# Strassen's seven products in two pieces of each down product of a hybrid decoder layer

## The chip, the cores and the metric

The kernel runs on 1 core of one Trainium2 chip. The metric is the device time of one execution, in microseconds (us). Three runs of the kernel before took 743.64 to 743.83 us, with a median of 743.7 us. The core has five engines with a queue of their own each: PE (TensorE, matmuls; its weight loads are listed as PEld), DVE (VectorE), ACT (ScalarE), POOL (GpSimd) and SP (SyncE, which here issues the loads of the weights). [...]

## The reference

One decoder layer on x of 1 x 256 x 1024, all F32. Three sub-layers follow each other, each between two RMS norms:

```python
def swiglu(x, w_gate, w_up, w_down):
    return (jax.nn.silu(x @ w_gate) * (x @ w_up)) @ w_down
...
h = h + 0.5 * rmsnorm(swiglu(rmsnorm(h, ffn1_pre_g), ffn1_w_gate, ffn1_w_up, ffn1_w_down), ffn1_post_g)
u = rmsnorm(h, mix_pre_g)
z, xbc, dt_raw, q, k, v, gate_logits = split(u @ w_in)
y_ssd = ssd_branch(z, xbc, dt_raw, ...)       # convolution, chunked state space (32 heads), gated norm, projection
y_att = diff_attn_branch(q, k, v, ...)        # differential attention, 8 heads, projection
h = h + rmsnorm((gates[0] * y_ssd + gates[1] * y_att) @ w_out, mix_post_g)
h = h + 0.5 * rmsnorm(swiglu(rmsnorm(h, ffn2_pre_g), ffn2_w_gate, ffn2_w_up, ffn2_w_down), ffn2_post_g)
```

The inner width of both SwiGLUs is 2816. The down product `@ w_down`, which the change touches, multiplies 256 x 2816 by 2816 x 1024.

## The kernel before

**Precision.** Every large product is made of fp32r matmuls. A value is split in two: `hi` is the value rounded to fp32r and `lo` is what is left. A product of two split values is taken as three matmuls, hi*hi, lo*hi and hi*lo. Weights are split on the way: ACT casts the F32 chunk to hi (`L168`), DVE subtracts hi from the chunk for lo (`L171`). Each chunk of 1 MB gives two pairs of such instructions, each of 128 x 1024.

**Weights.** All weights of the layer are listed in order of use as chunks of 128 partitions x 2048. SP loads them into three raw buffers (`load_to`, `L147`); a raw buffer goes back to SP when its last split has read it. `take()` hands the next chunk to the matmuls and sees to it that the splits of the two chunks behind it are written (`AHEAD = 3`). The split chunks live in tiles of 4 KB per partition of a pool called k4 (29 buffers), which also holds the activations, the gains and more. A pool k3 of 4 buffers of 3 KB holds tiles of the SSD branch (E) and of the attention (s); k2 (7 buffers of 2 KB) holds small ones. PSUM has 8 banks: 3 in the pool pj and 5 in the pool bg.

**A SwiGLU** (`ffn`). Gate and up products of 256 channels each (`mm_w`, into pj) are evicted by ACT and DVE, multiplied, and split into `gh` and `gl`, in which channels lie on partitions and the 256 tokens on the free axis. The down product (`mm_n`) then goes over 11 pieces of 256 channels, one weight chunk each. A piece is 24 matmuls of 128x128 by 128x512: 2 channel tiles, 2 token blocks, 3 terms, 2 halves of the outputs (`L470`). The four sums [token block][half] stay in four bg banks over all pieces. The last three pieces (`TAIL`) are held back, so that token block 0 is finished first: `ready(0)` then runs its norm (`post_norm`: square on ACT, product with the gain on DVE, rstd on POOL or ACT, addition to h on DVE) beside block 1's matmuls, and after the first SwiGLU the transposes for the next norm (`turned`, tile pu_mx) follow between block 1's matmuls.

**Order.** In the first products and in the tail of `mm_n` the order on some engines is that of the program (`own_order`). Elsewhere a planner decides, when the kernel is built, in which order each engine gets its instructions, from costs of its own. In the middle stage the work of the SSD branch and of the attention runs as background (`Background`): its pieces carry costs (`yield 1.4`) and come due while the projections z, q, k and the gates go on. At run time each engine works down its queue in the built order.

Of the kernel before, what the change touches and what calls it, by code (L numbers as in the profile page):

```python
# [11 lines left out]
F32 = mybir.dt.float32  # L15
# [9 lines left out]
P = 128  # L25
# [5 lines left out]
H_SSD = 32  # L31
H_ATT = 8
NEG = -1e30
K4_BUFS = 29
K3_BUFS = 4
K2_BUFS = 7
RAW_BUFS = 3
AHEAD = 3
# [3 lines left out]
BG_US = 3.15  # L42
GATE_US = 1.35
SSD_US = 1.55
BREAK, STOP = object(), object()


@with_exitstack
def tile_hybrid_layer(ctx: ExitStack, tc: tile.TileContext, x, ffn1_pre_g, ffn1_w_gate, ffn1_w_up,
# [33 lines left out]
    def bg(shape, name):  # L83
        return ps.tile(shape, F32, tag="bg", name=name, bufs=5)


    chunks = []

    def t_chunk(w, k0, c0):
        chunks.append((w[k0:k0 + D, c0:c0 + T].rearrange("(j p) c -> p j c", p=P), [P, KD, T]))  # L90

    def s_chunk(w, k0, c0):
        chunks.append((w[k0:k0 + 512, c0:c0 + 512].rearrange("(j p) c -> p j c", p=P), [P, 4, 512]))

    def n_chunk(w, k0):
        chunks.append((w[k0:k0 + 2 * P, :].rearrange("(j p) c -> p j c", p=P), [P, 2, D]))

    w_in2 = w_in[0]
    Z0, XS0, B0, C0, DT0, Q0, KK0, V0, G0 = 0, 2048, 4096, 4608, 5120, 5152, 6176, 7200, 8224
# [1 line left out]
    def ffn_chunks(wg, wu, wd):  # L101
        for w in (wg, wu):
            for k0 in (0, 512):
                s_chunk(w[0], k0, 0)
        for j in range(2, FF // T):
            t_chunk(wg[0], 0, j * T)
            t_chunk(wu[0], 0, j * T)
        for j in range(FF // T):
            n_chunk(wd[0], j * T)

    ffn_chunks(ffn1_w_gate, ffn1_w_up, ffn1_w_down)
    for c in range(2):
# [37 lines left out]
    def split_steps(ahead=True):  # L150


        i = len(splits)
        load_to(i + 1)
        r, shape = raws[i], chunks[i][1]
        nj = shape[1] // 2
        his, los = [], []
        splits.append((his, los))
        for q in range(2):
            hi = k4([P, nj, shape[2]], f"whi{i}{q}", F32R)  # L160
            lo = k4([P, nj, shape[2]], f"wlo{i}{q}", F32R)
            his.append(hi)
            los.append(lo)
            n = 1 if i == 0 else nj
            for j in range(0, nj, n):
                js = slice(j, j + n)
                copy = nc.scalar.copy if i + q + j else nc.vector.tensor_copy
                copy(hi[:, js, :], r[:, q * nj + j:q * nj + j + n, :])  # L168
                if not i + q + j:
                    yield  # L170
                nc.vector.tensor_sub(lo[:, js, :], r[:, q * nj + j:q * nj + j + n, :], hi[:, js, :].bitcast(F32))  # L171
                yield
        raws[i] = None
        if ahead:
            load_to(i + 1 + RAW_BUFS)

    def split_to(n):

        while len(splits) < min(n, len(chunks)):
            for _ in split_steps():  # L180
                pass

    def take(ahead=AHEAD):

        i = taken[0]
        taken[0] += 1
        split_to(i + ahead)
        his, los = splits[i]
        splits[i] = None
        nj = chunks[i][1][1] // 2  # L190
        return (lambda j: his[j // nj][:, j % nj, :], lambda j: los[j // nj][:, j % nj, :])

    def split(hi, lo, src):
# [259 lines left out]
        nc.gpsimd.dma_start(pg, v[0].partition_broadcast(P))  # L453
        return pg

    def mm_n(acc, acts, ready, turned, begun=lambda: None):


        n = len(acts) // 2
        held = []  # L460

        def one(i, w, parts):
            wh, wl = w
            for kt in range(2):
                ah, al = acts[2 * i + kt]
                for b, qs in parts:
                    ts = slice(b * P, (b + 1) * P)
                    for x_, w_ in ((ah, wh), (al, wh), (ah, wl)):
                        for q in qs:
                            nc.tensor.matmul(acc[b][q], x_[:, ts], w_(kt)[:, halves[q]],  # L470
                                             start=i == 0 and kt == 0 and x_ is ah and w_ is wh,
                                             stop=i == n - 1 and kt == 1 and w_ is wl)
                if i == 0:
                    begun()

        for i in range(n):
            w = take()
            if i < n - TAIL:
                one(i, w, ((0, (0, 1)), (1, (0, 1))))
            else:  # L480
                held.append((i, w))
        own_order(PE)
# [9 lines left out]
        split_to(taken[0] + AHEAD)  # L492
        ready(1)

    class Norm:

# [63 lines left out]
    def ffn(post_v, tag, ready, turned, then, products):  # L560
# [24 lines left out]
        back(1)  # L585
        del sgs
        then()
        for j in range(2, FF // T):
# [10 lines left out]
            nc.vector.tensor_tensor(sg, su, sg, ALU.mult)  # L599
            split(gh[:, o:o + 2, :], gl[:, o:o + 2, :], sg)  # L600
        if ready is store:
            act_table(EXP_LN)
        pg = load_gain(post_v, f"pg_{tag}")
        acc = [[bg([P, 512], f"acc_{tag}{b}{q}") for q in range(2)] for b in range(2)]
# [255 lines left out]
    cbm = [cbm2[g // 2][:, g % 2, :] for g in range(4)]  # L860

    def cb_work():
        for g in range(4):
            pc = bg([P, 3 * P], f"pcb{g}")
            nc.tensor.matmul(pc[:, P:], bT[:, g, :P], cT[:, g, :], start=True, stop=True)
            nc.tensor.matmul(pc[:, :P], bT[:, g, P:], cT[:, g, P:], start=True, stop=True)
            nc.vector.tensor_tensor(cbm[g], pc, m3.rearrange("p a b -> p (a b)"), ALU.mult)
            yield 0.5

# [207 lines left out]
    def att_work():  # L1077
# [4 lines left out]
        heads = [Head(hd, pairs[hd // 2]) for hd in range(H_ATT)]  # L1082
        for n in range(H_ATT // 2 + 2):
            here, old = heads[2 * n:2 * n + 2], heads[2 * n - 2:2 * n] if n else []
            for head in here:
                head.scores()
            for head in here:
                head.softmax()
                yield 2.3
            for head in old:  # L1090
                head.turn()
            if old and opens:
# [5 lines left out]
            if old:  # L1098
# [202 lines left out]
```

## Time and profile before

| what | value |
|---|---|
| median of 3 runs | 743.7 us |
| the profiled execution, and its span from first to last instruction | 743.95 us, 742.2 us |
| busy: PE / DVE / ACT / POOL | 734.1 / 525.2 / 441.1 / 38.0 us |
| first down product, from its first matmul | at 132.88 us |
| second down product, from its first matmul | at 676.16 us |
| granted TensorE clock, mean | 0.997 |

The page of the profile gives busy times by engine, the chain that ended last and the costliest groups of instructions. Every other view asks the same profiled execution: the chain in order of time has lines "start us, us, what"; the waits have lines "who waited <- for whom: us in total, times, longest us"; the timeline has lines "start us, us, engine, line, operation, out<-in xcount" and in brackets the idle time before it and what ended that. Lines such as L470 are lines of the kernel before.

### The profile page before, as it was taken

Reading aid. Unit: us, or ns where it says so; the run is one execution under the profiler, and the core shown is the slowest. Engines: PE = TensorE matmul, PEld = TensorE weight load, DVE = VectorE, ACT = ScalarE, POOL = GpSimd, SP = SyncE. Lnnn points to the kernel's source line nnn. Section 1 sums busy time; section 2 is a strip of 40 time slices with the busy share of each in tenths; the row PEclk is TensorE's granted clock in tenths of the full one; section 3 lists DMA queues with packets and bytes.
Section 4 is the critical chain, followed back from the end, with each engine's and each line's share of the span. In section 5 each row is a group of like instructions: output and inputs, shape, how many; then the busy total and the mean of one; then the engine's idle time right before and its main releaser. Section 6 shows DMA issues by size and latency. Waiting matters only on the chain.

```text
span 742.2 us, 11061 instructions
## 1 busy us (share of the span) xinstructions
PE 734.1 (99%) x4369; PEld 641.7 (86%) x4369; DVE 525.2 (71%) x807; ACT 441.1 (59%) x742; POOL 38.0 (5%) x72
## 2 busy tenths in 40 slices
PE   8999999999999999999999999999999999999996
PEld 7888888888889999999999888888888888888885
DVE  6986567654577888787878997684775857766612
ACT  6665557553566565959957656772664655665512
POOL 2700000000300000000000000000020000000000
PEclk9999999999999999999999999999999999999998
DMA  8884666487253647666556455374470777645701
GB/s 291 232 261 150 213 227 254 170 286 226 64 169 118 192 150 225 191 186 223 170 161 217 165 178 213 118 244 182 140 243 15 227 226 227 193 172 185 273 1 57
DMA packets 94212, 137.96 MB, mean 186 GB/s; under 512 B 2684, under 2 KB 68304, under 8 KB 94160
## 3 DMA queue, kind: packets, MB, share of 16 engines
q1 hardware_dynamic: 91488, 129.51, 53.0%
q0 software_dynamic: 2368, 7.22, 3.1%
q8 instruction: 34, 0.56, 0.3%
q10 hardware_dynamic: 304, 0.53, 0.2%
q14 instruction: 18, 0.15, 0.1%
HBM read 136.17 MB, written 1.08 MB: 185 GB/s over the span
## 4 chain that ended last, share of the span: by engine, by line
PE 98%; DMA 1%; issue 0%; DVE 0%; SPq 0%; DVEq 0%; ACT 0%
PE acc_f L470 16%; PE pup_f L219 9%; PE pg_f L219 9%; PE pws L234 6%; PE pgt L234 6%; PE pg_f L218 4%; PE pup_f L218 4%; PE pn_f L244 3%; PE pn_f L234 3%; PE acc_mx L470 3%; PE pn_mx L234 3%; PE pwd L234 3%; PE pz L205 2%; PE pxs L207 2%; PE pz L207 2%; PE pxs L205 2%
## 5 line engine op out<-in xcount | busy, mean ns | idle before, releaser
L171 DVE TENSOR_TENSOR wlo<-raw,whi 128x1024 fp32r<-128x1024 f32 (+1 forms) x246 | 291.0, 1212 | 56.1 <-ACT whi L168 54.8
L168 ACT CAST whi<-raw 128x1024 fp32r<-128x1024 f32 (+1 forms) x245 | 246.8, 1045 | 55.4 <-PE acc_f L470 19.6
L219 PE MATMUL pg_f<-u_f,whi 128*128 128x512 f32 x288 | 101.3, 396 | 0.0
L219 PE MATMUL pup_f<-u_f,whi 128*128 128x512 f32 x288 | 101.1, 396 | 0.0
L218 PE MATMUL pg_f<-u_f,wlo 128*128 128x256 f32 x252 | 70.6, 280 | 0.0
L218 PE MATMUL pup_f<-u_f,wlo 128*128 128x256 f32 x252 | 70.3, 279 | 0.0
L219 PEld LDWEIGHTS pg_f<-u_f,whi 128*128 128x128 f32 x288 | 52.8, 188 | 9.7
L219 PEld LDWEIGHTS pup_f<-u_f,whi 128*128 128x128 f32 x288 | 52.7, 188 | 9.8
L470 PE MATMUL acc_f<-whi,gh_f 128*128 128x512 f32 x176 | 58.2, 390 | 0.0
L470 PE MATMUL acc_f<-whi,gl_f 128*128 128x512 f32 x176 | 58.1, 389 | 0.0
L470 PE MATMUL acc_f<-wlo,gh_f 128*128 128x512 f32 x176 | 58.1, 389 | 0.0
L218 PEld LDWEIGHTS pg_f<-u_f,wlo 128*128 128x128 f32 x252 | 47.5, 189 | 1.8
L218 PEld LDWEIGHTS pup_f<-u_f,wlo 128*128 128x128 f32 x252 | 47.5, 189 | 1.6
L223 DVE TENSOR_TENSOR su_f<-pup_f,su_f 128x256 f32<-128x256 f32 x36 | 15.2, 422 | 40.4 <-ACT su_f L222 40.4
L470 PEld LDWEIGHTS acc_f<-whi,gl_f 128*128 128x128 f32 x176 | 33.0, 188 | 6.9
L470 PEld LDWEIGHTS acc_f<-wlo,gh_f 128*128 128x128 f32 x176 | 33.0, 188 | 6.8
L470 PEld LDWEIGHTS acc_f<-whi,gh_f 128*128 128x128 f32 x176 | 33.0, 188 | 6.8
L234 PE MATMUL pgt<-whi,u_mx 128*128 128x512 f32 x128 | 33.1, 393 | 0.0
L222 ACT COPY su_f<-pup_f 128x256 f32<-128x256 f32 x36 | 13.4, 372 | 31.4 <-PE pup_f L219 31.1
L204 PE MATMUL pxs<-u_mx,whi 128*128 128x256 f32 x128 | 31.7, 285 | 0.0
L205 PE MATMUL pz<-u_mx,whi 128*128 128x256 f32 x128 | 31.6, 284 | 0.0
L204 PE MATMUL pz<-u_mx,whi 128*128 128x256 f32 x128 | 31.6, 284 | 0.0
(310 smaller groups left out, 1432.7 us busy)
## 6 DMA issues: line engine op xcount, KB each, us to landing
raw<-in_w_in_dram SPq DMA_DIRECT2D x40, 1024.0 KB, 5.4
raw<-in_ffn_w_down_dram SPq DMA_DIRECT2D x22, 1024.0 KB, 5.5
raw<-in_ffn_w_gate_dram SPq DMA_DIRECT2D x20, 1024.0 KB, 5.7
raw<-in_ffn_w_up_dram SPq DMA_DIRECT2D x20, 1024.0 KB, 5.4
raw<-in_ssd_w_branch_dram SPq DMA_DIRECT2D x8, 1024.0 KB, 5.0
acb<-acd POOLq DMA_DIRECT2D x8, 512.0 KB, 5.3
raw<-in_da_w_branch_dram SPq DMA_DIRECT2D x4, 1024.0 KB, 5.1
raw<-in_w_out_dram SPq DMA_DIRECT2D x4, 1024.0 KB, 5.0
```

The costliest lines, as they stand in the source:

```text
L168: copy(hi[:, js, :], r[:, q * nj + j:q * nj + j + n, :])
L171: nc.vector.tensor_sub(lo[:, js, :], r[:, q * nj + j:q * nj + j + n, :], hi[:, js, :].bitcast(F32))
L204: nc.tensor.matmul(acc[m], wh(j)[:, cs], ah(k0 + j), start=first and j == ks[0], stop=False)
L205: nc.tensor.matmul(acc[m], wh(j)[:, cs], al(k0 + j), start=False, stop=False)
L207: nc.tensor.matmul(acc[m], wl(j)[:, cs], ah(k0 + j), start=False, stop=last and j == ks[-1])
L218: nc.tensor.matmul(acc[:, :T], wl(j)[:, cs], ah(j), start=False, stop=False)
L219: nc.tensor.matmul(acc, wh(j)[:, cs], ahl(j), start=j == 0, stop=j == KD - 1)
L222: nc.scalar.copy(dst[:, m, :], acc[:, T:])
L223: nc.vector.tensor_tensor(dst[:, m, :], acc[:, :T], dst[:, m, :], ALU.add)
L234: nc.tensor.matmul(acc, a(k0 + j), b(j), start=first and i == 0, stop=last and i == 11)
L244: nc.tensor.matmul(accs[b], x_(k0 + j), w_(j), start=first and j == 0 and w_ is wh and x_ is acts[b][0], stop=last and j == 3 and w_ is wl)
L470: nc.tensor.matmul(acc[b][q], x_[:, ts], w_(kt)[:, halves[q]], start=i == 0 and kt == 0 and x_ is ah and w_ is wh, stop=i == n - 1 and kt ...
```

## The change

A quad is two pieces of the down product taken together, 512 channels. As matrices, its activations (256 tokens x 512 channels) and weights (512 x 1024) are cut into quarters: two token blocks by two halves of the channels, two halves of the channels by two halves of the outputs. Strassen's algorithm (in Winograd's form) gives the four output blocks from seven products of sums of quarters instead of eight products of quarters. A product is 6 matmuls (2 channel tiles, 3 terms), so that a quad is 42 matmuls instead of 48. In each of the two SwiGLUs two quads are made (channels 512 to 1023 and 1024 to 1535), with a plain piece between them and six plain pieces after them.

- Weights (`class Quad`): a quad's two chunks give seven split operands instead of four. Three are quarters, four are sums of quarters (`sum_of`, one DVE subtract each). `units` is the list of what `take()` hands out: a chunk, or one product of a quad. A quad needs two raw buffers at a time, and gives one back when its quarters are used up.
- Activations (`sums_of`): while the gate and up products run, four sums per quad on DVE, and a split of them.
- Accumulation (`mm_quads`): products 2, 3, 4 and the plain block 8 stay in four bg banks and go on accumulating in `mm_n`; product 5 takes the fifth bg bank, products 1, 6, 7 the three pj banks. Both quads accumulate in the same banks.
- `combine`: after the quads, one ACT copy and four DVE adds make what the four output blocks still lack. `done(b)` adds it to the accumulated blocks, two DVE adds for each token block, and `post_norm` then reads the sum from SBUF instead of PSUM.
- Pools: k4 has 32 buffers, and the tiles of k3 come from k4.
- In the middle stage, the eight matmuls of `cb_work` are put side by side; the transposes (`turn`) of attention pairs 0 and 1 stand ahead of the next scores; one cost is 2.7 instead of 2.3 from the fourth round on.

```diff
-K4_BUFS = 29
-K3_BUFS = 4
+K4_BUFS = 32
+QUADS = (1, 2)
+FIRST, LAST = (1, 2, 3, 5, 7, 6, 4), (1, 6, 7, 2, 5, 3, 4)
...
     def k3(shape, name, dt=F32):
-        return sb.tile(shape, dt, tag="k3", name=name, bufs=K3_BUFS)
+        return k4(shape, name, dt)
...
+    class Quad:
+        PLAIN = {1: 0, 2: 2, 3: 3}
+        SUMS = {5: (1, 0), 6: (3, 5), 7: (3, 1), 4: (2, 6)}
...
+        def give_back(self):
+            for j in range(2):
+                if raws[self.i + j] is not None and not self.uses[2 * j] and not self.uses[2 * j + 1]:
+                    raws[self.i + j] = None
+                    load_to(self.i + j + 1 + RAW_BUFS)
+
+        def sum_of(self, p):
+            if p not in self.sums:
+                n, m = self.SUMS[p]
+                m = self.sum_of(m) if p in (6, 4) else self.quarter(m, p)
+                t = k4([P, 2, 512], f"wt{self.i}{p}")
+                nc.vector.tensor_sub(t, self.quarter(n, p), m)
+                self.sums[p] = t
+            return self.sums[p]
+
+        def split(self, p):
+            load_to(self.i + 2)
+            hi = k4([P, 2, 512], f"wqh{self.i}{p}", F32R)
+            src = self.quarter(self.PLAIN[p], p) if p in self.PLAIN else self.sum_of(p)
+            nc.scalar.copy(hi, src)
+            lo = k4([P, 2, 512], f"wql{self.i}{p}", F32R)
+            last_lo[0] = nc.vector.tensor_sub(lo, src, hi.bitcast(F32)).ins
+            self.give_back()
+            return lambda kt: hi[:, kt, :], lambda kt: lo[:, kt, :]
...
+    def ahead_of(i, n):
+        n *= 4
+        while n > 0 and i < len(units):
+            n -= 4 if units[i][1] is None else 1
+            i += 1
+        return i
...
-        split_to(i + ahead)
+        split_to(ahead_of(i, ahead))
...
+    def sums_of(g, even, odd):
+        bs = (slice(0, P), slice(P, T))
+        v, hi, lo = (k4([P, 4, 2, P], f"s{n}{g}", dt) for n, dt in (("v", F32), ("h", F32R), ("l", F32R)))
+        nc.vector.tensor_tensor(v[:, 0], even[:, :, bs[1]], odd[:, :, bs[1]], ALU.add)
+        nc.vector.tensor_sub(v[:, 2], even[:, :, bs[0]], even[:, :, bs[1]])
+        nc.vector.tensor_sub(v[:, 1], v[:, 0], even[:, :, bs[0]])
+        nc.vector.tensor_sub(v[:, 3], odd[:, :, bs[0]], v[:, 1])
+        split(hi, lo, v)
+        return hi, lo
+
+    def mm_quads(acts, sums, tag):
+        bank = {p: bg([P, 512], f"acc_{tag}p{p}") for p in (2, 3, 5, 4, 8)}
+        bank.update({p: pj(f"acc_{tag}p{p}") for p in (1, 6, 7)})
+        acc = [[bank[2], bank[3]], [bank[4], bank[8]]]
...
+            sh, sl = sums[j]
+            for p in LAST if last else FIRST:
+                wh, wl = take()
+                for kt in range(2):
...
+                    for x_, w_ in ((ah, wh), (al, wh), (ah, wl)):
+                        mm(p, x_, w_(kt), last and kt == 1 and w_ is wl)
...
+        def combine():
+            nc.scalar.copy(p1, bank[1])
+            m = add(u2, bank[6], p1)
+            tc.add_manual_dep(m.ins, last_lo[0].name, order, reason="behind the last quad's weights")
+            add(u3, bank[7], u2)
+            add(u4, bank[5], u2)
+            add(c4, bank[5], u3)
...
         def done(b):
-            post_norm(b, acc[b], pg, 4.0, tag, ready is store)
+            for q in range(2):
+                nc.vector.tensor_tensor(rest[b][q], acc[b][q], rest[b][q], ALU.add)
+            post_norm(b, rest[b], pg, 4.0, tag, ready is store)
             ready(b)
 
-        mm_n(acc, gu, done, turned)
+        mm_n(acc, gu, done, turned, pairs=[j for kind, j in down[2 * len(QUADS) - 1:]], begin=False,
+             taken_all=combine)
...
     def cb_work():
-        for g in range(4):
-            pc = bg([P, 3 * P], f"pcb{g}")
...
+        pcs = [bg([P, 3 * P], f"pcb{g}") for g in range(4)]
...
+            if 3 <= n <= H_ATT // 2:
+                pairs[n - 3].turn()
             for head in here:
                 head.scores()
             for head in here:
                 head.softmax()
-                yield 2.3
+                yield 2.3 if n < 3 else 2.7
...
-            if n >= 2:
+            if n >= H_ATT // 2:
                 pairs[n - 2].turn()
```

More of the change, by code (lines that the diff above doesn't have):

```diff
@@ L95, in n_chunk, with quad @@
     def n_chunk(w, k0):
-        chunks.append((w[k0:k0 + 2 * P, :].rearrange("(j p) c -> p j c", p=P), [P, 2, D]))
+        chunk(w[k0:k0 + 2 * P, :].rearrange("(j p) c -> p j c", p=P), [P, 2, D])
+    def quad(w, k0, products):
+        n = len(units)
+        for k in (k0, k0 + 2 * P):
+            n_chunk(w, k)
+        del units[n:]
+        q = Quad(len(chunks) - 2, products)
+        units.extend((q, p) for p in products)
+    plain = [j for j in range(FF // T) if j // 2 not in QUADS]
+    down = []
@@ L98, in tile_hybrid_layer @@
+    for g in QUADS:
+        down.append(("quad", g))
+        if g != QUADS[-1]:
+            down.append(("plain", plain.pop(0)))
+    down += [("plain", j) for j in plain]
     w_in2 = w_in[0]
@@ L107, in ffn_chunks @@
             t_chunk(wu[0], 0, j * T)
-        for j in range(FF // T):
-            n_chunk(wd[0], j * T)
+        for kind, j in down:
+            if kind == "quad":
+                quad(wd[0], j * 2 * T, LAST if j == QUADS[-1] else FIRST)
+            else:
+                n_chunk(wd[0], j * T)
     ffn_chunks(ffn1_w_gate, ffn1_w_up, ffn1_w_down)
@@ L150, in split_steps @@
     def split_steps(ahead=True):
-        i = len(splits)
+        i, _ = units[len(splits)]
         load_to(i + 1)
@@ L177, in split_to @@
     def split_to(n):
-        while len(splits) < min(n, len(chunks)):
+        while len(splits) < min(n, len(units)):
+            of, p = units[len(splits)]
+            if p is not None:
+                splits.append(of.split(p))
+                continue
             for _ in split_steps():
                 pass
+    def ahead_of(i, n):
[4 more added lines that the diff above has]
+        return i
     def take(ahead=AHEAD):
@@ L481, in mm_n @@
                 held.append((i, w))
+        taken_all()
         own_order(PE)
@@ L587, in ffn @@
         then()
+        sums = {}
         for j in range(2, FF // T):
```

79 lines of the change are left out of this document (66 added, 13 removed).

## The prediction

> **What bounds the kernel now.** I read the page's busy shares first, then the chain that ended last, then what PE (TensorE) waited for, then the chain in order of time around the two down products.
>
> ```profile
> PE 734.1 (99%) x4369; PEld 641.7 (86%) x4369; DVE 525.2 (71%) x807; ACT 441.1 (59%) x742; POOL 38.0 (5%) x72
> ...
> PE 98%; DMA 1%; issue 0%; DVE 0%; SPq 0%; DVEq 0%; ACT 0%
> ```
> ```profile
> PE warm L310 <- POOL ident L296: 1.6, 1, 1.6
> PE pn_f L244 <- DVE whi L168: 0.2, 1, 0.2
> ```
> ```profile
> 132.88 55.77 PE acc_f L470 x246
> 188.64 0.88 PE pu_mx L355 x8
> ...
> 676.16 59.87 PE acc_f L470 x264
> ```
> ```profile
> 133.00:190.00 57.00, 57.00 (x257) 47.31 (x256) 33.65 (x32) 29.09 (x39) 1.74 (x4) 1.00 0.67 221
> 676.00:736.00 60.00, 60.00 (x265) 49.36 (x263) 26.67 (x28) 21.60 (x28) 0.00 (x0) 1.00 0.31 114
> ```
>
> The kernel is one uninterrupted stream of matmuls: PE has 98% of the chain and waits 1.8 us in the whole run, at the start. A matmul that goes is worth its pitch, as long as the stream stays whole. In the second down product 264 matmuls take 59.87 us, 0.227 us each; the 389 ns of a single record overlap. In the two windows (PE, PEld, DVE (VectorE), ACT (ScalarE), POOL, then the granted clock) the clock is 1.00, and DVE and ACT are about half busy. So there is room on them in the mean. Whether it lies where the new work needs it decides this change.
>
> **What goes.** A quad of two pieces was 48 matmuls and becomes 42. Four quads: 24 matmuls by 0.227 = 5.4 us less on the path, 2.7 us per down product. The built program agrees: 24 matmul instructions fewer, none elsewhere.
>
> **What comes on DVE and ACT in a quad.** Splitting a chunk's half is one ACT cast (hi) and then one DVE subtract (lo) of 128x1024. Before, two pieces took 4 of each; now 7 products take 7 of each and 4 weight sums of the same size, on DVE. How these run in the first down product, before:
>
> ```profile
> 128.84 1.28 ACT L254 ACT_TABLE_LOAD   x1
> ...
> 130.27 0.35 ACT L222 COPY su_f<-pup_f 128x256 f32<-128x256 f32 x1
> 132.91 0.38 ACT L222 COPY su_f<-pup_f 128x256 f32<-128x256 f32 x1 [2.29 <-PE pup_f L219]
> 134.56 0.62 ACT L194 CAST gh_f<-sg_f 128x512 fp32r<-128x512 f32 x1 [1.27 <-DVE sg_f L599]
> 135.09 5.79 ACT L168 CAST whi<-raw 128x1024 fp32r<-128x1024 f32 x6
> 143.64 2.00 ACT L168 CAST whi<-raw 128x1024 fp32r<-128x1024 f32 x2 [2.76 <-DMA raw<-in_ffn_w_down_dram]
> 146.79 2.00 ACT L168 CAST whi<-raw 128x1024 fp32r<-128x1024 f32 x2 [1.15 <-DMA raw<-in_ffn_w_down_dram]
> ```
> ```profile
> 133.32 0.42 DVE L223 TENSOR_TENSOR su_f<-pup_f,su_f 128x256 f32<-128x256 f32 x1 [2.24 <-ACT su_f L222]
> 133.78 0.69 DVE L599 TENSOR_TENSOR sg_f<-su_f,sg_f 128x512 f32<-128x512 f32 x1
> 135.22 0.69 DVE L195 TENSOR_TENSOR gl_f<-sg_f,gh_f 128x512 fp32r<-128x512 f32 x1 [0.74 <-ACT gh_f L194]
> 136.17 6.90 DVE L171 TENSOR_TENSOR wlo<-raw,whi 128x1024 fp32r<-128x1024 f32 x6 [0.26 <-ACT whi L168]
> ```
>
> Six casts in 5.79 us are 0.97 each, six subtracts in 6.90 are 1.15 each. A sum of F32 halves is the same operation on the same size: I take 1.15 (the 128x512 rows with F32 and with fp32r outputs both show 0.69, so the output type costs nothing). A quad on DVE is then 11 x 1.15 = 12.7 us against 42 x 0.227 = 9.5 us on PE, where before it was 4.6 against 10.9. A sum product also goes DVE (sum), ACT (hi), DVE (lo), and where the next DVE row is that lo, DVE stands for the cast: 1.05 plus the handovers (0.09 from DVE's 134.47 to ACT's 134.56 above, 0.04 back), some 1.25 with the drain of the sum.
>
> I laid the built order of the changed kernel end to end with these durations. PE would do quad 1 from 133.1 to 142.6, the piece between (24 x 0.227) to 148.1, quad 2 to 157.6; the seventh product of quad 2 (product 4) is due at 156.2. On ACT the table load now stands behind the su_f copy of 130.27, so the cast for product 7 of quad 1 ends near 133.2. From about 133.3 DVE's queue holds, in this order: 18 operations of 1.15 (two lo and one sum of quad 1's products 7 and 6, sum and lo of 4, the two lo of the piece between, then 7 lo and 4 sums of quad 2) = 20.7; su_f, sg_f and gl_f = 1.7; and four places where the lo stands right behind its own sum (4 of quad 1; 6, 7 and 4 of quad 2) = 5.0. That is 27.4 us: the hi of the last product comes at 160.0, its lo at 161. The first quad is still in time (its product 4 at 141.6, due at 141.3 with its third matmul 0.45 later). In quad 2, product 7's hi comes at 152.9 and is due at 150.8, product 4's at 160.0 against 156.2. PE loses 3.6 us there and some 0.4 for the lo: 4.0 in all, in several waits of up to 1.4 us. The second down product has the same order and the same sum.
>
> Bounds of this wait: 0 if the queue runs 4.3 us ahead of where I laid it, 5.3 if each of some 13 handovers costs 0.1 us more. I take 4.0 per down product, by the rows of handovers above. The tiles these operations write come free as PE finishes quad 1, by the built waits each before DVE's turn; price 0, and up to one product (1.4 us) a time if not. So each down product gains 2.7 and loses 4.0: **+1.3, twice +2.6 us**.
>
> [...]
>
> **Other parts of the down products.** The activation sums (four adds of 128x256, a split of 128x1024, twice per product) fall into the gate/up stage:
>
> ```profile
> 88.50:132.90 44.40, 44.40 (x255) 38.69 (x255) 29.76 (x40) 26.85 (x42) 0.53 (x1) 1.00 0.56 201
> ```
>
> DVE works 29.76 of 44.40 us there. 4 x 0.42 (the su_f row, also 128x256) + 1.15 = 2.8 us per quad fit in the 14.6 free; price 0, and 2.8 each if that cover were gone. The five `combine` operations (3 us on DVE) fall beside the six last pieces; price 0 by the half-idle windows. At the end of each block `done` puts an add of 128x512 ahead of the square, 0.6 us by the pitch of these rows:
>
> ```profile
> 736.78 0.69 DVE L440 TENSOR_TENSOR og_f<-acc_f,pg_f 128x512 f32<-128x512 f32 x1 [3.33 <-ACT jp_f L341]
> 737.38 1.41 DVE L449 SCALAR_TENSOR_TENSOR h<-og_f,rp_f,h 128x512 f32<-128x512 f32 x2
> ```
>
> The last add has no cover: **+0.6 us**. In the first product the transposes wait for block 0's h:
>
> ```profile
> 185.32 0.69 DVE L440 TENSOR_TENSOR og_f<-acc_f,pg_f 128x512 f32<-128x512 f32 x1 [3.39 <-ACT jp_f L341]
> 186.46 1.41 DVE L449 SCALAR_TENSOR_TENSOR h<-og_f,rp_f,h 128x512 f32<-128x512 f32 x2 [0.45 <-POOL rp_f L347]
> ```
>
> h is done at 187.87 and needed at 188.64: 0.8 us of slack. In the new order the add and two subtracts for the next weights (raw35, raw36) stand ahead of h on DVE: 0.6 + 2 x 1.15 = 2.9, less the slack and the 0.45 idle ahead of h: 1.6 if the square and rstd cover nothing more. Those subtracts also wait for their loads, which quad 2 made late (SP gives a raw buffer back only after the last sum has read it) and which land 3.2 us apart (143.64 and 146.79 above), so they catch up only 2.2 us per piece of 5.4. Between 0 and 4 (more than one load behind); **+1.0 us**, near the lower end because six pieces lie between. The gain pg is loaded by POOL after the quads and used some 20 us later: 0.
>
> **The middle.** E and s tiles move into the k4 pool, and the planner places the py products of an SSD group later. For group 2 they stood after 30 matmuls of pq0 and now stand after 45 of pk0: 63 matmuls of 0.12 = 7.6 us later. Behind them on DVE and ACT:
>
> ```profile
> 350.29 2.75 PE py L913 x32
> ...
> 369.69 0.96 PE pk L207 x8
> ```
> ```profile
> 352.56 1.65 DVE L920 SCALAR_TENSOR_TENSOR xs<-xs,cols_b,py 128x256 f32<-128x256 f32 x4
> 354.12 2.35 DVE L927 TENSOR_TENSOR xs<-xs,sz 128x1024 f32<-128x1024 f32 x2
> ...
> 357.76 1.28 DVE L882 TENSOR_TENSOR X<-px,dt 128x512 f32<-128x512 f32 x2
> ...
> 361.22 0.87 DVE L898 TENSOR_SCALAR E<-acb,acs 128x128 f32<-128x128 f32 x4
> ```
> ```profile
> 356.97 1.98 ACT L168 CAST whi<-raw 128x1024 fp32r<-128x1024 f32 x2
> ...
> 361.79 0.63 ACT L261 ACTIVATE E<-E 128x512 f32<-128x512 f32 x1 [1.66 <-DVE E L898]
> 362.33 1.27 ACT L261 ACTIVATE E<-acb,acs 128x128 f32<-128x128 f32 x4
> ```
>
> Before, ACT casts the weights of pk1 at 356.97, ahead of group 3's E. Now the cast stands behind E's. py ends 7.6 us later, at 360.5 (its first half at 359.1); DVE needs 1.65 + 2.35 + 1.15 + 1.28 + 0.4, some 6.6, until E's input is there (365.7 to 367.1); ACT then needs 0.63 + 1.27 + 0.63 and the cast, some 3.2 with overlaps: 368.9 to 370.3. pk1 is due at 367.8 (the row at 369.69 follows its first 16 matmuls of 0.12). A wait of 1.1 to 2.5; **+1.8 us**. The attention turns that move ahead of the scores need a PSUM bank which the fourth score tile takes next: 0 to 1, **+0.4**. The four cb products put side by side are the same matmuls: 0, between -0.6 (three fewer returns) and +0.5 (a later conv).
>
> **The sum.** -5.4 + 8.0 (quads) + 0.6 (end) + 1.0 (first tail) + 1.8 + 0.4 (middle) = +6.4 us. The profiled execution took 743.95 us (span 742.2), 0.25 above the median of 743.7. Predicted: 743.95 + 6.4 = 750.4, as a median **750.1 us**. A measurement of this kernel tells 0.2%, 1.5 us, from no change.
>
> **Rivals.**
> - *The lead holds (faster).* For: the half-idle windows, and splits run two pieces ahead. Against: the 27.4 us queue. It decides at 4.3 us: if product 4's weights of quad 2 are there by 156.6, no wait is left. Then -5.4 + 0.6 and 0 to 2.2 in the middle: 739.2 to 741.4, say 740.
> - *Only the quads wait.* The quads lose what I say, the first tail and the middle nothing: -5.4 + 8.0 + 0.6 = +3.2, 747; with 3 us lost per down product, 745. For it: both waits are shorter than 2 us and hang on one row's place.
> - *The loads do not catch up.* The first tail waits 4 us, the quads 5.3 each: 756. For it: three raw buffers, two held by a quad. Against: the DMA engines are 0.67 and 0.31 busy in the two windows. -5.4 + 10.6 + 0.6 + 4.0 + 2.2 = +12.
> - *The clock falls.* A wait long enough lets the granted clock drop; then matmuls of 0.45 us (twice 0.227) follow for a while. The rows show 1.00 in all windows above, so no price but this: each 3 us at half speed cost 1.5; with two such places 753. [...]
>
> **Chances.** The forecast 0.62 (its own range 748 to 754), the lead holds 0.10, only the quads wait 0.14, the loads 0.12, the clock 0.02. The range reaches down into the second rival and up to the third: 744.5 to 756. Faster by over 0.2%: the first rival, 0.10. Within 0.2%: the low edge of the second, 0.03. Slower: 0.87.
>
> **What would show it.** Matmuls 24 fewer. In quad 2 of each down product PE waits for wqh/wql tiles, some 4 us, on the chain; DVE nearly full from 133 to 161 with "<-ACT wqh" gaps near 1.1 us. A wait of pu_mx for h of about 1 us, of pk1 for whi near 1.8 us. Wrong if PE's waits in quad 2 are under 1 us per down product (the lead held), if DVE's sums take other than 1.15 us, or if pk1 does not wait.

## The result and the profile after

| | before | after |
|---|---|---|
| median of the runs | 743.77 us | 756.95 us |
| lowest to highest | 743.64 to 743.92 | 754.29 to 758.29 |
| profiled execution (span) | 743.95 (742.2) | 754.29 (752.6) |

The changed kernel is slower: ratio 1.0172, 95% interval 1.016 to 1.0184. The forecast was 750.1, in a range of 744.5 to 756.0, so the time lies just above the range. Its runs differ by 4 us, those of the kernel before by 0.3 here (by up to 2.4 in the later sets), and the profiled execution is the shortest of the four: its granted clock is 0.997, that of the others 0.993 to 0.994. So the trace explains +10.4 us of span (752.6 - 742.2), and some 2.7 us of the median stand outside it.

First the page's busy shares of the kernel after, to be held against the row of before in the prediction (PE 734.1, DVE 525.2 us):

```profile
PE 734.0 (98%) x4345; PEld 636.9 (85%) x4345; DVE 577.8 (77%) x871; ACT 456.2 (61%) x760; POOL 39.3 (5%) x72
```

24 matmuls are gone, as forecast, and DVE has 52.6 us more. PE's busy sum does not show the saving: the end of each matmul is modelled some 0.16 us past the start of the next (0.39 against a pitch of 0.227), and each stop adds that to the sum, which makes up a part of it. What PE waited for, in the kernel after (us in total, times, longest):

```profile
PE pu_mx L444 <- DVE h L538: 2.1, 1, 2.1
PE acc_f1p L608 <- ACT wqh L128: 1.8, 3, 1.0
PE acc_f2p L608 <- ACT wqh L128: 1.8, 3, 1.0
PE warm L399 <- POOL ident L385: 1.6, 1, 1.6
PE pk L293 <- ACT whi L242: 1.5, 2, 1.3
PE psc L1155 <- DVE ol L1242: 1.0, 1, 1.0
PE acc_f2p L608 <- DVE wql L130: 0.4, 1, 0.4
PE acc_f1p L608 <- DVE wql L130: 0.4, 1, 0.4
PE pq L296 <- DVE wlo L245: 0.3, 1, 0.3
...
```

Before, the list held the warm-up and one wait of 0.2. All the waits that the prediction named are here. What they cost is read better from where the stages begin, because this view counts a wait from the modelled end of the last matmul. The first starts of these tiles on PE, from both timelines (pg_f is that of the last gate piece before the first down product):

| stretch | before, us | after, us | difference |
|---|---|---|---|
| start to pg_f | 121.53 | 121.27 | -0.26 |
| pg_f to pu_mx (first down product, first tail) | 66.95 | 70.61 | +3.66 |
| pu_mx to pn_mx | 5.02 | 5.33 | +0.31 |
| pn_mx to pq (projections, cb) | 153.03 | 153.07 | +0.04 |
| pq to pgt (pk1 and group 3) | 53.26 | 56.02 | +2.76 |
| pgt to pwd (attention) | 105.13 | 106.87 | +1.74 |
| pwd to pn_f | 46.40 | 46.38 | -0.02 |
| pn_f to the end (second down product, end) | 190.88 | 193.05 | +2.17 |

That adds up to +10.40. Less the -2.72 of the matmuls (12 x 0.227), and less the 0.6 for the add at the end, the last row leaves 4.3 us for the quads of the second product. In the first product 3.66 + 2.72 - 4.3 leaves 2.1 for the wait of pu_mx, which is what the list of waits says. So the terms are: quads 8.6, first tail 2.4 (2.1 and the 0.31 behind it), pk1 2.8, attention 1.7, end 0.6, matmuls -5.4.

DVE's timeline of the kernel after, in quad 2 of the first product (wt is a sum, wql a lo):

```profile
146.14 1.23 DVE L120 TENSOR_TENSOR wt<-raw,wt 128x1024 f32<-128x1024 f32 x1
148.53 1.23 DVE L130 TENSOR_TENSOR wql<-wt,wqh 128x1024 fp32r<-128x1024 f32 x1 [1.17 <-ACT wqh L128]
149.68 1.22 DVE L120 TENSOR_TENSOR wt<-raw,raw 128x1024 f32<-128x1024 f32 x1
152.00 1.23 DVE L130 TENSOR_TENSOR wql<-wt,wqh 128x1024 fp32r<-128x1024 f32 x1 [1.11 <-ACT wqh L128]
...
156.55 1.22 DVE L120 TENSOR_TENSOR wt<-raw,wt 128x1024 f32<-128x1024 f32 x1
158.94 1.23 DVE L130 TENSOR_TENSOR wql<-wt,wqh 128x1024 fp32r<-128x1024 f32 x1 [1.17 <-ACT wqh L128]
```

After each of the three sums DVE stands for the ACT cast, 1.11 to 1.17 us (forecast some 1.25), with operations of other products queued behind. The last lo ends at 160.2 (forecast 161).

### The profile page after: what moved, and what is told of

Same layout as the page of the kernel before. It is cut to its first block, busy times and chain, and to the rows that moved or that the text cites. A ratio compares the mean times of both kernels' runs of the same rounds, so it can differ in the third digit from the quotient of the medians.

```text
span 752.6 us, 11085 instructions
## 1 busy us (share of the span) xinstructions
PE 734.0 (98%) x4345; PEld 636.9 (85%) x4345; DVE 577.8 (77%) x871; ACT 456.2 (61%) x760; POOL 39.3 (5%) x72
## 5 line engine op out<-in xcount | busy, mean ns | idle before, releaser
L245 DVE TENSOR_TENSOR wlo<-raw,whi 128x1024 fp32r<-128x1024 f32 (+1 forms) x230 | 271.4, 1211 | 23.9 <-ACT whi L242 23.2
L242 ACT CAST whi<-raw 128x1024 fp32r<-128x1024 f32 (+1 forms) x229 | 229.7, 1042 | 26.6 <-DMA raw<-in_ffn_w_down_dram 11.9
L128 ACT CAST wqh<-wt 128x1024 fp32r<-128x1024 f32 x16 | 16.8, 1049 | 27.8 <-DVE wt L120 27.7
L293 PE MATMUL pxs<-u_mx,whi 128*128 128x256 f32 x128 | 31.5, 284 | 0.0
L294 PE MATMUL pxs<-u_mx,whi 128*128 128x256 f32 x128 | 31.4, 283 | 0.0
L130 DVE TENSOR_TENSOR wql<-wt,wqh 128x1024 fp32r<-128x1024 f32 x16 | 19.6, 1225 | 13.5 <-ACT wqh L128 13.3
L323 PEld LDWEIGHTS pgt<-whi,u_mx 128*128 128x128 f32 x128 | 23.6, 188 | 5.4 <-DVE gt L1378 0.3
L993 DVE SCALAR_TENSOR_TENSOR xs<-pxs,cols_b,xs 128x255 f32<-128x255 f32 (+2 forms) x48 | 22.1, 478 | 7.4 <-ACT xs L990 6.9
L350 ACT ACTIVATE s<-s,nm 128x128 f32<-128x128 f32 (+1 forms) x32 | 14.2, 445 | 18.0 <-DVE nm L1165 10.4
```

The costliest lines, as they stand in the source:

```text
L128: nc.scalar.copy(hi, src)
L130: last_lo[0] = nc.vector.tensor_sub(lo, src, hi.bitcast(F32)).ins
L293: nc.tensor.matmul(acc[m], wh(j)[:, cs], ah(k0 + j), start=first and j == ks[0], stop=False)
L294: nc.tensor.matmul(acc[m], wh(j)[:, cs], al(k0 + j), start=False, stop=False)
L323: nc.tensor.matmul(acc, a(k0 + j), b(j), start=first and i == 0, stop=last and i == 11)
L993: nc.vector.scalar_tensor_tensor(dst[:, m, s:], acc[:, m, :T - s], cw(3 - s, c), dst[:, m, s:], ALU.mult, ALU.add)
```

## The experiments

My theory after the result: the loss has separate causes (the quads' round trips on in-order queues, the late loads ahead of the first tail, the merged pool at pk1, the place of the attention turns at psc), and the rest is drops of the clock. The rivals are that the loads hold the quads up, that one cause makes the others, or that a wait of 2 us cannot touch the clock. Each ratio below is to runs of the kernel before on the same chip, whose medians were 743.8 to 744.25. A stretch of 3.4 us at half speed (in "pool only" three windows of 2.5 us from 7.5 us on show 0.88, 0.50 and 0.94) costs up to 1.7; the start (up to pg_f) differs by up to 3 us between executions (121.27 us in the kernel after, 124.24 in "pool only"), from waits there (1.5 us of pn_f for whi in "quads only") and such stretches. Where a profile is compared with another, the start is taken off.

**Quads only.** From the changed kernel, the middle put back:

```diff
-K4_BUFS = 32
+K4_BUFS = 29
+K3_BUFS = 4
...
     def k3(shape, name, dt=F32):
-        return k4(shape, name, dt)
+        return sb.tile(shape, dt, tag="k3", name=name, bufs=K3_BUFS)
...
-            if 3 <= n <= H_ATT // 2:
-                pairs[n - 3].turn()
...
-                yield 2.3 if n < 3 else 2.7
+                yield 2.3
...
-            if n >= H_ATT // 2:
+            if n >= 2:
```

The loop of the cb products is as before too.

> The quads as in the changed kernel, the middle as before: the k3 tiles have their pool of four again (k4 has 29 buffers) and the cb products and attention turns stand in their old order. Changed kernel, profiled: +10.3 us of span. Its milestones put +4.0 into the first down product with its tail, +4.5 into pk1 and the attention turns, +2.2 into the second down product and the end. If these parts are independent, +5 to +6 is left here: 749 to 750 us with a granted clock of 0.997; pk1 and psc do not wait, wqh and wql are waited for some 4 us per down product. If the clock falls on account of the quads and of the first tail, 752 to 753 with 0.993 in most runs; if the wait of pk1 is what lets it fall, 0.997 in all. Rival (the quads cost nothing, all of the loss lies in the middle and the clock): 739 to 741.

750.38 us (749 to 750 expected), ratio 1.0083 (1.0068 to 1.0098), clocks 0.996 to 0.998. Its waits:

```profile
PE acc_f2p L609 <- ACT wqh L129: 1.8, 3, 1.0
PE acc_f1p L609 <- ACT wqh L129: 1.8, 3, 1.0
...
PE pu_mx L445 <- DVE h L539: 0.5, 1, 0.5
```

The same waits in the quads, none at pk and psc. From pg_f to pu_mx it takes 68.99 us, +2.04 on before: -2.72 + 0.5 + 4.3 for the quads. The rest of the span is +2.1 from pn_f to the end, 2.0 lost at the start, with a drop of the clock there (the mean is 0.996), and 0.4 behind the first tail. The quads' cost stands alone, and that of the first tail is not a fixed amount: 0.5 here, 2.1 in the changed kernel.

**Middle only.** The kernel before, with the shared pool, the cb loop and the turns of the changed one:

```diff
-K4_BUFS = 29
+K4_BUFS = 32
...
-        return sb.tile(shape, dt, tag="k3", name=name, bufs=K3_BUFS)
+        return k4(shape, name, dt)
...
+            if 3 <= n <= H_ATT // 2:
+                pairs[n - 3].turn()
...
-                yield 2.3
+                yield 2.3 if n < 3 else 2.7
...
-            if n >= 2:
+            if n >= H_ATT // 2:
```

> The kernel before, with the middle of the changed one alone: k3 tiles in the common k4 pool of 32, the four cb products side by side, the attention turns ahead of the scores. No quads. My theory: pk1 waits for whi and psc for DVE as in the changed kernel, +2.7 to +4.6 us: 746.5 to 748.4. Rival (the waits of the middle come from work that the quads made late, not from the pool and the order): 743.5 to 744.5, no wait at pk1. On the clock: if the wait of pk1 (1.3 us at the longest) lets it fall, 0.993 in some runs and up to 3 us more; if not, 0.997 in all.

749.2 us, 0.8 above the 746.5 to 748.4 that my theory gave, ratio 1.0076 (1.006 to 1.0092); the profiled execution is the shortest (748.45, span 746.7 at a clock of 0.999). Its waits:

```profile
PE pk L203 <- ACT whi L167: 1.5, 2, 1.3
PE psc L990 <- DVE ol L1077: 1.0, 1, 1.0
```

The same waits as in the changed kernel, with no quad in the program. pq to pgt takes 56.03 us, pgt to pwd 106.84. The two halves cost 6.6 and 5.4 us by their medians, 12.0 together against 13.2 measured with both.

**Pool only.** The kernel before with the first two edits of the run above alone.

> The kernel before with the k3 tiles in the common k4 pool of 32, and nothing else: no quads, the old order of cb and of the attention turns. It splits the +4.7 of the middle alone. My theory: the merged pool moves py of group 2 and gives the whole wait of pk1 (+2.0 to +2.8), nothing at psc: 746 to 746.8. Rival (the order of the turns gives it all): 743.5 to 744.3 and no wait of pk1.

748.44 us, ratio 1.0056 (1.0038 to 1.0075). The profile has the wait of pk (1.5 in two) and none of psc; pq to pgt takes 56.01 us and pgt to pwd 105.12. So the pool makes the whole +2.75 of the first stretch. The +1.7 of the second comes from the other edits of "middle only"; that it is the order of the turns, and not the cb loop or the cost of 2.7, is read from its place (psc, behind the turns) and was not tried by itself. The median came out above the 746 to 746.8 expected: 2.7 us of the profiled span went at the start, with 3.4 us at half speed from 9.4 on in it.

**Sum ahead.** The changed kernel; each sum goes one lo earlier into DVE's queue, into the time in which DVE stood:

```diff
     class Quad:
...
         def __init__(self, i, products):
...
+            self.next = dict(zip(products, products[1:]))
...
             nc.scalar.copy(hi, src)
+            if self.next.get(p) in self.SUMS:
+                self.sum_of(self.next[p])
             lo = k4([P, 2, 512], f"wql{self.i}{p}", F32R)
```

> The changed kernel with one edit: the weight sum of the next product is issued on DVE ahead of the lo of this product, so that DVE has work while ACT casts hi. The same operations, the same loads, the same buffers. My theory (the quads lose to round trips DVE sum, ACT hi, DVE lo on in-order queues): the four round trips of 1.25 us per down product go, the waits for wqh and wql in quad 2 fall from 4 us to under 1 in each down product, and the time to 744 to 747 us. Rival (the loads or the bare number of DVE operations hold the quads up): the waits stay at 3 us or more per down product, 753 or more.

745.26 us, ratio 1.002 (1.0011 to 1.003). The list of waits has no wqh, no wql and no pu_mx, as expected (under 1 us; 744 to 747 us). DVE's timeline in quad 2:

```profile
144.37 1.22 DVE L121 TENSOR_TENSOR wt<-raw,raw 128x1024 f32<-128x1024 f32 x1
145.51 2.48 DVE L133 TENSOR_TENSOR wql<-wt,wqh 128x1024 fp32r<-128x1024 f32 x2
...
150.18 1.22 DVE L121 TENSOR_TENSOR wt<-raw,wt 128x1024 f32<-128x1024 f32 x1
151.31 1.22 DVE L133 TENSOR_TENSOR wql<-raw,wqh 128x1024 fp32r<-128x1024 f32 x1
152.57 1.23 DVE L133 TENSOR_TENSOR wql<-wt,wqh 128x1024 fp32r<-128x1024 f32 x1
```

No idle time for a cast, and the last lo ends at 153.8 instead of 160.2. The same operations cost 4 us less per down product when their order changes: pg_f to pu_mx takes 64.54, -2.41 on before, against the -2.72 of the matmuls. The work on DVE, 12.7 us per quad, was not too much; its order was.

**Four raw buffers.** The changed kernel:

```diff
-K4_BUFS = 32
+K4_BUFS = 30
...
-RAW_BUFS = 3
+RAW_BUFS = 4
```

> The changed kernel with four raw buffers for the weights in place of three (k4 has 30 buffers in place of 32 for them). The order of the work on DVE and ACT in the quads stays as it is. My theory (round trips of in-order queues): the waits for wqh and wql stay at 3 us or more of 4 in each down product; the first tail's wait for h (2.1 us), which I lay to loads that quad 2 made late, goes: 754 to 755.5, the two k4 buffers fewer put aside. Rival (the loads do not catch up): the waits of the quads go too, to under 1 us in each down product: 747 or less.

753.11 us, ratio 1.0127 (1.0109 to 1.0144). My expectation for the quads fell: their waits did not stay at 3 us or more.

```profile
PE psc L1155 <- DVE ol L1242: 3.6, 1, 3.6
...
PE acc_f1p L608 <- ACT wqh L128: 0.7, 1, 0.7
PE acc_f2p L608 <- ACT wqh L128: 0.7, 1, 0.7
```

pg_f to pu_mx takes 66.05: -0.90, that is -2.72 and 1.8 left for the quads. DVE still stands 1.1 to 1.2 us at each round trip, but its queue runs 2.3 us earlier (the lo behind the last sum starts at 156.66, not at 158.94). ACT's timeline around the second pair of quad 1 says why, after first, then with four buffers:

```profile
121.09 1.05 ACT L128 CAST wqh<-raw 128x1024 fp32r<-128x1024 f32 x1 [2.03 <-DMA raw<-in_ffn_w_down_dram]
```
```profile
118.94 2.00 ACT L128 CAST wqh<-raw 128x1024 fp32r<-128x1024 f32 x2
```

With three buffers the quad's second chunk comes 2 us late, and the whole queue behind it starts late. So the lateness has two parts, and either remedy works by its own size: 4.3 - 2.3 = 2.0 us should be left with earlier loads (1.8 measured), and nothing where the round trips (3 x 1.15 in quad 2, more in quad 1) are gone. The loads were a part of the cause that I had not named; they were not all of it, as the rival had it. The first tail's wait is gone, as expected. psc waited 3.6 in place of 1.0, and the matmuls of 128x512 behind it stand some 0.43 us apart until about 482, 0.227 after that, so that pgt to pwd takes 4.9 more than in the changed kernel; whether that is the price of two k4 buffers fewer was not tried by itself.

**The changed kernel again**, for what its runs differ by.

> The changed kernel again, beside the same runs of the kernel before, to see what its runs differ by. The sum of its two halves run alone, by their profiled spans less the drop of clock at the start of the first one (748.8 - 2.0 - 742.0 = +4.8, 746.7 - 742.0 = +4.7), and 0.9 for the first tail, is 752.4 of span without a drop, 754.1 in all. If the rest of the measured 757 is drops of the clock of some 1.7 us each, the runs stand 1.7 us apart or so, those with a mean clock lower by 0.002 are 1.7 us longer, and the profile shows the drop after a wait of PE.

756.47 us, ratio 1.017 (1.0156 to 1.0184), spans 752.2 to 758.5; the shortest stands where the sum without a drop put it (752.4). The profiled one is the longest. Its windows around the first tail's wait (3.2 us here, 2.1 in the first trace) and around that of psc (1.0); columns as in the prediction, the clock third from last:

```profile
191.40:194.70 3.30, 0.15 (x1) 0.00 (x0) 2.51 (x5) 1.18 (x3) 2.00 (x2) 1.00 0.78 238
194.80:198.10 3.30, 3.30 (x12) 3.01 (x13) 2.88 (x7) 2.91 (x11) 0.00 (x0) 0.50 0.35 123
```
```profile
481.50:484.80 3.30, 2.29 (x17) 1.51 (x16) 3.30 (x7) 2.50 (x5) 0.00 (x0) 1.00 0.27 51
485.00:488.20 3.20, 3.20 (x8) 2.44 (x8) 3.20 (x5) 1.52 (x9) 0.00 (x0) 0.50 0.64 248
```

Behind each of the two waits the clock is at one half for some 3.4 us, and matmuls of 128x512 stand 0.43 us apart. Against the first trace, pg_f starts 1.8 later, pg_f to pu_mx takes 1.05 more, pu_mx to pn_mx 1.4 more (the first drop), pgt to pwd 1.6 more (the second), nothing else moves by more than 0.04: 5.9, the difference of the spans. The order of the runs goes by the clock only in part (754.8 at 0.998, 754.7 at 0.993), so something else varies as well; in the profiled run it is the start and the first tail's wait, and of the others no trace was kept.

**The clock alone.** A program of nothing but a stream of matmuls of 128x512 that stops 20 times for each of eight lengths (`dose` holds the widths of the DVE operations in the chain, `m` runs from 38 to 44, and the next matmul reads w):

```diff
+    for d, dose in enumerate(DOSES):
...
+        for i in range(m):
+            nc.tensor.matmul(acc, a, w, start=i == 0, stop=i == m - 1)
+        src = acc
+        for i, c in enumerate(dose):
+            dst = w if i == len(dose) - 1 else v[i]
+            nc.vector.scalar_tensor_tensor(out=dst[:, :c], in0=src[:, :c], scalar=0.0, in1=h[:, 1, :c],
+                                           op0=ALU.mult, op1=ALU.add)
+            src = dst
```

> Nothing of the layer is computed: it loads x, runs a stream of matmuls of 128x512 (fp32r) and stores, and its time has nothing to do with the layer's. The stream stops 160 times: after 38 to 44 matmuls (some 9.3 us) TensorE waits for a chain of DVE operations that starts from its own last result. Eight stages of 20 equal waits, longer from stage to stage, from some 0.4 to some 3 us. It measures the price of a wait in clock. [...] Theory B (from the drops seen after the 1.3 us wait of pk1 and the 2.7 us wait of pu_mx: half speed for about 3.4 us, begun some 1 us after the wait): the clock is 1.00 in the first stages, and from a wait of 1 to 1.5 us on a share of the waits is followed by a drop, a share that grows with the wait; a stage of which every wait has a drop shows a mean clock near 0.85.

One execution was profiled. Waits and windows of the last four stages, in order (the first four have waits up to 1.1 us and a clock of 1.00):

```profile
PE acc L40 <- DVE w L44: 26.2, 20, 1.3
...
PE acc L40 <- DVE w L44: 30.2, 20, 1.5
...
PE acc L40 <- DVE w L44: 40.7, 20, 2.0
...
PE acc L40 <- DVE w L44: 51.2, 19, 2.7
```
```profile
838.00:1047.00 209.00, 182.81 (x781) 144.90 (x781) 23.67 (x40) 0.00 (x0) 1.00 0.00 1
1056.00:1270.00 214.00, 183.80 (x785) 145.43 (x784) 27.67 (x40) 0.00 (x0) 1.00 0.00 0
1278.00:1524.00 246.00, 205.26 (x796) 160.99 (x795) 37.53 (x60) 0.00 (x0) 0.92 0.00 0
1530.00:1792.00 262.00, 206.72 (x784) 162.24 (x782) 51.07 (x82) 0.00 (x0) 0.90 0.00 0
```

No drop up to 1.5 us; from 2.0 us on the mean clock falls. By estimate, with a drop of 3.4 us at half speed as in the layer, 0.08 x 246 x 2 / 3.4 is some 12 drops after 20 waits of 2.0 us, and 0.10 x 262 x 2 / 3.4 some 15 after 19 of 2.7. The rival that a wait of 2 us cannot touch the clock falls. Of theory B the share that grows with the wait holds; its border of 1 to 1.5 us is too low.

**The clock by kinds of matmuls.** The same, with 128x256 matmuls (first four stages) and with F32 matmuls of 64 rows on both sides of the wait (last four).

> Again nothing of the layer is computed, and its time is not the layer's: a stream of matmuls that stops 160 times for a chain of DVE operations, with the kinds of matmuls that stand around the waits of pk and of psc. Stages 1 to 4: 76 to 88 matmuls of 128x256 between waits of some 1.0, 1.3, 1.5 and 1.7 us (as at pk). Stages 5 to 8: 34 to 40 matmuls of 128x512, and on both sides of the wait two groups of four F32 matmuls of 64 rows (as at psc), waits of some 0.9 to 1.6 us. In the first dose run no wait up to 1.51 us let the clock fall, and of those of 2.04 us 12 in 20 did, though in the layer it fell after waits of 1.33 (pk) and 1.01 us (psc). If the kind of the matmuls counts (a matmul that fills less of the array, or has longer pauses around it, counts as less activity), drops appear below 1.5 us in stages 5 to 8, perhaps in 3 and 4. If only the length of the wait counts, none below 1.8 us in any stage; then what let the clock fall at pk and psc stays open.

The waits came out up to 0.2 us longer or shorter than expected. The stages with 128x256 and waits of 1.6 and 1.9 us, and the last with 64 rows (1.7):

```profile
475.00:702.00 227.00, 195.00 (x1590) 191.52 (x1589) 27.65 (x40) 0.00 (x0) 1.00 0.00 1
711.00:962.00 251.00, 214.10 (x1602) 210.21 (x1601) 33.48 (x60) 0.00 (x0) 0.92 0.00 1
...
1751.00:2012.00 261.00, 227.13 (x1324) 178.73 (x1321) 28.94 (x62) 0.00 (x0) 1.00 0.00 1
```

Every stage shows 1.00 but the one of 1.9 us, where 0.08 x 251 x 2 / 3.4 is some 12 drops after 19 waits. So the border lies, in these two executions, between 1.5 and 2.0 us with 128x512 and between 1.6 and 1.9 with 128x256; the stages with 64 rows, up to 1.7, do not reach it. No kind of matmul brought a drop below 1.9 us. What let the clock fall behind the waits of 1.3 (pk, once in the six traces with that wait: 0.50 from 368.9 to 372.2 us in "sum ahead") and 1.0 us (psc, once in four traces) stays open.

**Sum ahead, old middle.** The edits of "sum ahead" and of "quads only" together.

> The sum issued ahead, as in the run before, and with it the middle of the kernel before (own k3 pool, old order of cb and attention). If the three causes are all there is: -5.4 us for 24 matmuls, +0.6 for the add at the end, 0 to 1 at the first tail and in the quads: 739 to 741 us at a clock of 0.997, faster than both kernels. If the saved matmuls are worth less than 0.227 us each, or the clock falls in runs without a wait near 2 us too: 742 to 745.

741.52 us, ratio 0.9967 (0.9957 to 0.9977): faster than before, but 0.5 us above the 739 to 741 expected. The profiled run, its longest, waits 2.7 us for h in the first tail and runs some 3.4 us at half speed behind it:

```profile
186.90:190.20 3.30, 0.70 (x5) 0.46 (x5) 2.10 (x4) 1.28 (x5) 0.88 (x2) 1.00 0.93 290
190.30:193.60 3.30, 3.30 (x11) 2.72 (x11) 2.71 (x9) 3.30 (x13) 1.15 (x2) 0.50 0.11 34
```

**Sum ahead, old middle, four raw buffers** (`RAW_BUFS = 4`, `K4_BUFS = 27`).

> The version with the sum ahead and the old middle, with four raw buffers in place of three (k4 has 27 buffers in place of 29 for them). The run before it lost 2.7 us to the first tail's wait for h and 1.7 to the clock behind it. If late loads make that wait, it goes, and what is left is -5.4 for the matmuls, +0.6 for the add at the end and some 0.5 in the quads: a span of 737.7, 739 to 740 us, with all runs within 1.5 us of each other. If the wait stays (then DVE's order alone makes h late), 741 to 743 as with three buffers.

739.57 us, ratio 0.9934 (0.992 to 0.9947); five runs from 739.25 to 740.29, the profiled span 737.7 as expected. PE's list of waits has one line left:

```profile
PE warm L403 <- POOL ident L389: 1.6, 1, 1.6
```

The wait for h is gone with the fourth raw buffer, so late loads made it. The time is 4.7 us less than before (744.25 beside it; 3.9 to 6.0 by the interval), which fits the -5.4 of the matmuls and the +0.6 of the add. So a removed matmul is worth about its 0.227 us once nothing waits.

## Why the prediction was wrong

Its direction and the places of its waits held. Two steps failed: the waits of the first tail, of pk1 and of the attention turns were sized too small, and the clock was priced at nothing. The first alone would have left the time inside the range: the first trace of the changed kernel has all these waits, shows no drop of the clock while PE has matmuls (1.00 up to 747, 0.58 from there to the end), and took 754.29 us.

- **Matmuls, -5.4.** Right within the interval of the last experiment.
- **Quads, 8.0.** Right in place and kind, 8.6 measured. The four DVE-ACT-DVE round trips are shown by "sum ahead": the sum of 149.68, which stood behind the lo that waited 1.17 us for its cast, runs there in such a gap. So DVE kept the built order, on which the term rests. Incomplete: I took the queue's start near 133.3 as given, and 2.3 us of its lateness came from a chunk that waited for its raw buffer. The working is also a little off in itself: product 4's hi at 160.0, due at 156.2, is 3.8 us, not 3.6.
- **First tail, 1.0 (0 to 4).** Mis-sized: 2.4 in the first trace, 3.5 in the second. I counted two subtracts ahead of h and put the value near the lower end "because six pieces lie between". DVE's timeline after has three between the first og_f and h, and two of their three casts waited for a load:

```profile
185.60 1.22 DVE L245 TENSOR_TENSOR wlo<-raw,whi 128x1024 fp32r<-128x1024 f32 x1
186.74 0.68 DVE L769 TENSOR_TENSOR u_f<-acc_f1p,u_f 128x512 f32<-128x512 f32 x1
187.34 1.22 DVE L245 TENSOR_TENSOR wlo<-raw,whi 128x1024 fp32r<-128x1024 f32 x1
188.47 0.69 DVE L529 TENSOR_TENSOR og_f<-u_f,pg_f 128x512 f32<-128x512 f32 x1
189.07 1.22 DVE L245 TENSOR_TENSOR wlo<-raw,whi 128x1024 fp32r<-128x1024 f32 x1
191.08 1.41 DVE L538 SCALAR_TENSOR_TENSOR h<-og_f,rp_f,h 128x512 f32<-128x512 f32 x2 [0.79 <-POOL rp_f L436]
```

  What h waits for last is rp_f on POOL, whose length I had taken as unchanged. Its first operation, before and then after:

```profile
185.46 0.31 POOL L346 TENSOR_SCALAR rp_f<-sp_f 128x1 f32<-128x1 f32 x1 [62.94 <-ACT jp_f L341]
```
```profile
188.82 1.57 POOL L435 TENSOR_SCALAR rp_f<-sp_f 128x1 f32<-128x1 f32 x1 [31.23 <-ACT jp_f L430]
```

  It takes 1.3 us more and ends 0.1 us behind the third subtract. The two operations of rp_f took 0.88 us before (0.31 + 0.57) and 2.14 in the first trace (1.57 + 0.57); POOL's column has 2.00 for two in the window of the second trace (191.40:194.70) and 0.88 in that of "sum ahead, old middle" (186.90:190.20). So the subtracts cost twice: they hold the add of u_f, and one of them lies beside rp_f. This is read from the traces and was not tried by itself.
- **pk1, 1.8 (1.1 to 2.5).** Mis-sized: +2.76. The waits that the list shows at pk and pq are 1.8 together, but every stop costs more than the list says. In quad 2 a wait listed as 0.40 put the next matmul 0.79 us behind the last one (149.02 to 149.81), 0.56 above the pitch of 0.227, and the one after it came 0.34 later, 0.11 above it: some 0.27 per stop of such matmuls. Three stops at pk and pq at that price bring the 1.8 to 2.6.
- **Attention turns, 0.4 (0 to 1).** Mis-sized: 1.7. I let the score tile wait for a bank but did not add up what frees it. In "middle only" ACT's oh (473.59, 0.68) and DVE's ol (475.15, 0.74) must end first, and the scores follow directly behind the transposes that oh and ol read.
- **End add, 0.6, and cb, 0.** The end was not measured alone; in the last experiment pn_f to the end is 1.9 us shorter than before, against -2.72 + 0.6 = -2.1. pn_mx to pq moved by 0.04.
- **The clock, priced at 0, chance 0.02.** The step that took the time out of the range. It went by a longest wait of 1.4 us, where 2.1 to 3.2 came, and no run shows that waits up to 1.4 us always leave the clock alone in the layer: drops stood behind waits of 1.3 (pk) and 1.0 us (psc), though the two dose runs show none up to 1.7 us. In the first set the three runs without a trace have a clock lower by 0.003 to 0.004, by estimate 2.3 to 3.0 of 755 us, and are 2.0 to 4.0 us longer than the traced one.

  That a wait lets the clock fall in some executions and not in others is seen, and what decides it was not shown: the wait of 2.1 us in the first trace has 1.00 behind it (191.8 to 198.0), that of 3.2 us in the second has 0.50, and in the dose runs some 12 of 20 waits of 2.0 us and 15 of 19 of 2.7 us were followed by a drop, by the estimate from the mean clock.

The miss of 6.8 us (756.95 - 750.1) is 4.0 of mis-sized terms (quads 0.6, tail 1.4, pk1 0.95, attention 1.3, less 0.25 at the start), and the rest is what varies from run to run, by the estimate above mostly the clock. "The loads do not catch up", which set the range's upper end at 756, came in part: at the tail, and in the queue's start.

## What to carry to other kernels

When work is added to engines that are half idle, lay out their queues in order and look for operations that stand right behind their own input's producer on another engine; putting one independent operation between them was worth 4 us per down product here, at no cost. Ask too what sets the time at which that queue starts. For a stream of matmuls, count every forecast wait at its listed time plus the restart (0.27 us a stop here), and any wait near 2 us as one that may cost another 1.7 us in clock (by estimate, behind 12 of 20 waits of 2.0 us here).

## What was not expected of the hardware

By estimate from the mean clock, a stop of TensorE of 1.9 to 2.0 us was followed by 3.4 us at half clock in 12 of 20 cases (128x512) and in 12 of 19 (128x256), one of 2.7 us in 15 of 19; after stops of up to 1.7 us the mean stayed at 1.00 in the two dose runs. In the layer drops were seen behind waits of 1.0 and 1.3 us as well, which these runs do not explain.
